# Up projection: the high and the low half of the activations side by side in one 512-column matmul, in two of seven product slots

## The chip, the cores and the metric

The kernel runs on one core of one Trainium2 chip. The metric is the device time of one execution in microseconds (us); the kernel before takes 685.49 us, the median of three runs (685.24 to 686.26).

## The reference

One layer of a decoder trunk on 512 tokens of width 1024 (`SEQ = 512`, `D_MODEL = 1024`, `D_FF = 2816`): two attention branches, a merge, and then the gated MLP whose first matrix product is the one that is changed here.

```python
def _conv_ffn(h, w_up, conv_w, conv_b, w_down):
    u = h @ w_up                       # (512, 1024) @ (1024, 5632)
    a, g = jnp.split(u, 2, axis=-1)    # 2816 columns each
    s = a.shape[1]
    ap = jnp.pad(a, ((0, 0), (CONV_WIDTH - 1, 0), (0, 0)))
    a = ap[:, 0:s] * conv_w[0] + ap[:, 1:s + 1] * conv_w[1] + ap[:, 2:s + 2] * conv_w[2] + conv_b
    return (jax.nn.gelu(a, approximate=False) * g) @ w_down
...
    h2 = _rmsnorm(x, norm2_g[l]) * (1.0 + scale2) + shift2
    x = x + gate2 * _conv_ffn(h2, w_up[l], conv_w[l], conv_b[l], w_down[l])
return _rmsnorm(x, final_g)
```

All arrays are float32.

## The kernel before

The kernel computes the float32 products with float32r matmuls. Every operand is split into a high part (a cast to float32r on ScalarE) and a low part (the rest, a subtraction on VectorE), and a product is three matmuls: high weights times high activations, high weights times low activations, low weights times high activations. In the up projection the weights are the stationary operand, 128x128 each, and the activations are the moving operand, 256 tokens wide (H = 256).

The up projection is a Strassen-Winograd scheme. It works on 11 pairs J = 0 to 10 of 128-column blocks (NPR = 11). For each J the four blocks of weights are the upper and lower half of the 1024 rows for the `a` columns and for the `g` columns, and the four blocks of activations are the two halves of the rows for tokens 0 to 255 ("lo") and 256 to 511 ("hi"). Instead of eight block products there are seven, called p1, m5, m6, p2, m7, p3, p4, and they are issued in this order: one slot each. A slot has, for u = 0 and u = 1 (128 of the pair's 256 output columns each), 4 steps over the rows times 3 matmuls: 24 matmuls in all (`mul_slot`). Then `behind(J, name)` reads the result out of the accumulator memory (PSUM):

- p1 (L1394): ScalarE copies it to `a[lo]`. m5 (L1396): ScalarE copies it to `g2`. m6 (L1398): it has been added onto p1 in PSUM; ScalarE copies the sum to `a[hi]`.
- p2 (L1400): VectorE adds it to `a[lo]`. m7 (L1402): it has been added onto p1 + m6; VectorE subtracts it from `g2`. p3 (L1404): it has been added onto m5; VectorE adds the sum to `a[hi]`. p4 (L1406): it has been added onto p1 + m6 + m7; VectorE multiplies it into the result.

After p3 come the convolution and GELU of this pair (`conv`: bias on ScalarE L1369, two taps on VectorE L1373 and L1374, GELU on ScalarE L1377). At each slot the weights of a later slot are made ready (`prep`): for m6 and p3 a sum of two blocks (L1293, VectorE), then the cast (L1299, ScalarE), then the low part (L1303, VectorE). The high and low weight tiles have three buffers each (WB = 3), so a cast for one slot can start when the slot three before it has been multiplied.

A PSUM bank holds 128 x 512 float32, and an accumulator of the up projection takes half a bank. For each u there are four banks, and `psum(J, name)` says which one a product goes to and in which half of it (h):

```python
    def psum(J, name):
        if name in ("m5", "p3"):
            b, h = bV, J % 2
        elif name == "p2":
            b, h = bX, J % 2
        else:
            b, h = (bU0, bU1)[J % 2], J // 2 % 2
        return [b[u][:, h * H : (h + 1) * H] for u in range(2)]
```

For J = 0, for J = 1 and for the slot p1 of J = 2 the order on VectorE, ScalarE, TensorE and GpSimd is written out by hand: there `mul_slot(2, "p1")` is followed by `mul_slot(1, "p4")`, and `behind(2, "p1")` stands behind `cast_w(2, "m6")`. From the slot m5 of J = 2 on the compiler's scheduler orders the engines: it takes instructions that are ready, those that stand earlier in the program first.

Of the kernel before, what the change touches and what calls it, by code (L numbers as in the profile page):

```python
# [8 lines left out]
F32 = mybir.dt.float32  # L9
F32R = mybir.dt.float32r  # L10
AF = mybir.ActivationFunctionType
# [3 lines left out]
P = 128  # L15
D = 1024
S = 512
# [43 lines left out]
def kernel(  # L61
# [22 lines left out]
    nc = tc.nc  # L84
# [3 lines left out]
    def pool(name, bufs=1, space=None, stack=ctx):  # L88
        kw = {} if space is None else {"space": space}
        return stack.enter_context(tc.tile_pool(name=name, bufs=bufs, reuse_waits="tile", **kw))  # L90

    cpool = pool("const")
    big = pool("big")
# [6 lines left out]
    def fbank(name):  # L100
        return bank("f", 2, [P, S], name)

    def sbank(name, shape=(P, S)):
        return bank("s", 3, list(shape), name)
# [4 lines left out]
    def vbank(name):  # L109
        return bank("v", 1, [P, S], name)  # L110
# [97 lines left out]
        rstd_end(dst, *rstd_start(ssq, n, d, wpool, plus), n, wpool)  # L208


    def parts_of(n):
        a = big.tile([P, 6, S], F32R, tag=f"h{n}A", name=f"hT{n}A")
        b = big.tile([P, 2, S], F32R, tag=f"h{n}B", name=f"hT{n}B")
        return [a[:, k] for k in range(6)] + [b[:, k] for k in range(2)]

    hTh, hTl = parts_of("h"), parts_of("l")
    p1 = ExitStack()
    pp = pool("p1", stack=p1)
    xn = pp.tile([P, NT, D], F32, name="xn")
# [408 lines left out]
    hT = (hTh, hTl)  # L628
# [427 lines left out]
    for s in range(4 * DIFF_HEADS):  # L1056
        h, n = divmod(s, NT)
# [164 lines left out]
            done(t)  # L1222


    bh = big.tile([P, 3, 4, 256], F32R, tag="hhA", name="bh")
    bl = big.tile([P, 3, 4, 256], F32R, tag="hlA", name="bl")
    braw = {}
    oacc = eight("oc")
    wa1 = gpart(2, [P, 2, 4, 256], "wa1")
# [26 lines left out]
    NPR, H = FT // 2, S // 2  # L1256
# [9 lines left out]
    W, R = {}, {(1, f"a1{h + 1}"): wa1[:, h] for h in range(2)}  # L1266
# [58 lines left out]
    with tc.issue_after(first_low[1].ins):  # L1325
# [6 lines left out]
    bU0 = [fbank("up0"), fbank("up1")]  # L1332
    bX = [sbank("up2"), sbank("up3")]
    bU1 = [sbank("up4"), vbank("up5")]
    bV = []
    T = dict(
        p1=(bh[:, 0], bl[:, 0]), p2=(bh[:, 1], bl[:, 1]), p3=(bh[:, 2], bl[:, 2]),
        m5=(tt[0][:, 0], tt[0][:, 1]), m6=(tt[1][:, 0], tt[1][:, 1]), m7=(tt[2][:, 0], tt[2][:, 1]),
        p4=(tt[3][:, 0], tt[3][:, 1]),
    )  # L1340


    def psum(J, name):
        if name in ("m5", "p3"):
            b, h = bV, J % 2
        elif name == "p2":
            b, h = bX, J % 2
        else:
            b, h = (bU0, bU1)[J % 2], J // 2 % 2
        return [b[u][:, h * H : (h + 1) * H] for u in range(2)]  # L1350

    av = {}

    def mul_slot(J, name, us=(0, 1)):
        o = psum(J, name)
        wh, wl = W[J, name]
        bh_, bl_ = T[name]
        for u in us:
            cu = slice(u * P, (u + 1) * P)
            for k in range(4):  # L1360
                for x, (w, b) in enumerate(((wh, bh_), (wh, bl_), (wl, bh_))):
                    nc.tensor.matmul(  # L1362
                        o[u], w[:, k, cu], b[:, k], start=name in ("p1", "m5", "p2") and k == 0 and x == 0,
                        stop=k == 3 and x == 2, skip_group_check=True,
                    )

    def conv_bias(J, u):
# [16 lines left out]
    def behind(J, name):  # L1384
        o = [] if name == "c22" else psum(J, name)
        g2 = g22[:, J % 2] if name in ("m5", "m7", "c22") else None
        if name == "p1":
            av[J] = big.tile([P, 2, S], F32, tag=("hhB", "hlB")[J % 2], name=f"a{J}")
        a = av[J]
        lo, hi = slice(0, H), slice(H, S)  # L1390
        for u in range(2):
            cc = grow(2 * J + u)
            if name == "p1":
                nc.scalar.copy(a[:, u, lo], o[u])  # L1394
            elif name == "m5":
                nc.scalar.copy(g2[:, u], o[u])  # L1396
            elif name == "m6":
                nc.scalar.copy(a[:, u, hi], o[u])  # L1398
            elif name == "p2":
                nc.vector.tensor_add(a[:, u, lo], a[:, u, lo], o[u])  # L1400
            elif name == "m7":
                nc.vector.scalar_tensor_tensor(g2[:, u], g2[:, u], -1.0, o[u], ALU.mult, ALU.subtract)  # L1402
            elif name == "p3":
                nc.vector.tensor_add(a[:, u, hi], a[:, u, hi], o[u])  # L1404
            elif name == "p4":
                nc.vector.scalar_tensor_tensor(cc[:, lo], o[u], -1.0, cc[:, lo], ALU.mult, ALU.mult)  # L1406
            elif name == "c22":
                nc.vector.tensor_mul(cc[:, hi], cc[:, hi], g2[:, u])
        if name == "p4":
            nc.vector.tensor_sub(grow(2 * J)[:, hi], grow(2 * J + 1)[:, hi], grow(2 * J)[:, hi])  # L1410
# [138 lines left out]
    for g in (2, 3):  # L1549
        tps[g] = turn2(0, g)  # L1550
    mul_slot(0, "p1")
    early(2, "vec")
    norm_a(3)
# [6 lines left out]
    early(2, "lo")  # L1560
    early(3, "lo")
    mul_slot(1, "p1", (0,))
    bt = gpart(0, [P, 2, 4, 256], "braw2")
    b12, b22 = bt[:, 0], bt[:, 1]
# [8 lines left out]
    def grow(j):  # L1573
        return gT[j // 4][:, j % 4]
# [5 lines left out]
    g22 = pairs2.rearrange("p (b u n) -> p b u n", b=2, u=2)  # L1580
    tps = {g: turn2(2, g) for g in (0, 1)}
    mul_slot(0, "p2", (0,))
    for g in (0, 1):
        for kk in range(2):
# [20 lines left out]
    for q in (q0, q1):  # L1605
        V.scalar_tensor_tensor(t1n[:, q], t1n[:, q], -1.0, b22[:, q], ALU.mult, ALU.subtract)
        hi_t(1, t1n, q)
    behind(0, "p1")
    nc.scalar.copy(bh[:, 2], b22)
    lo_t(1, t1n, q0)  # L1610
# [3 lines left out]
    cast_w(0, "p3")  # L1614
    V.tensor_sub(bl[:, 2], b22, bh[:, 2].bitcast(F32))
    behind(0, "m5")
    low_w(0, "p3")
    mul_slot(0, "p3")
# [3 lines left out]
    V.scalar_tensor_tensor(b21, t1n, -1.0, b21, ALU.mult, ALU.subtract)  # L1622
    hi_t(3, b21)
    behind(0, "m6")
    low_w(0, "m7")
    lo_t(2, b12)
# [116 lines left out]
        cbuf[c][:, x : x + (2 if g < 5 else 1) * S].rearrange("p (q n) -> p q n", n=S)  # L1743
        for g, (c, x) in enumerate(((0, 0), (0, 1024), (1, 0), (2, 0), (2, 1024), (3, 0)))
    ]
    s2 = big.tile([P, NPR, H], F32, tag="hhA", name="s2")
    s4 = big.tile([P, NPR, H], F32, tag="hlA", name="s4")

    second = {g: big.tile([P, 2, S], F32, tag=t, name=f"b22_{g}") for g, t in enumerate(("hhB", "hlB"))}
    m1 = pairs2.rearrange("p (t n) -> p t n", n=S)  # L1750
# [309 lines left out]
```

## Time and profile before

| | |
|---|---|
| time, median of 3 runs | 685.49 us (685.24 to 686.26) |
| span of the profiled execution, first to last instruction | 684.1 us |
| PE (TensorE matmul) busy | 675.3 us, 99% of the span |
| DVE (VectorE) busy | 564.2 us, 82% |
| ACT (ScalarE) busy | 384.5 us, 56% |
| matmuls of the up projection, line L1362 | first at 348.2 us, last at 571.6 us |
| mean granted TensorE clock | 0.998 |

The page gives the span of the profiled execution and no time of its own beside it; the median of the runs is 1.4 us longer than that span. PE is the matmul row, PEld the load of stationary weights, which runs beside it. In a timeline each line has the start in us, the duration in us, the engine, the line of the kernel, the operation, the tile written and the tiles read, the shapes, the number of merged instructions, and in brackets the idle time of the engine just before and what ended it. The matmuls are pipelined: the duration of one is longer than the distance to the next, and it is the distance that adds up.

### The profile page before, as it was taken

How to read it: one execution, taken by the hardware profiler on the slowest of the kernel's cores; microseconds unless marked ns; L12 is line 12 of the kernel's file. 1: busy time of each engine (PE TensorE's matmuls, PEld its weight loads, DVE VectorE, ACT ScalarE, POOL GpSimd, SP SyncE). 2: the span in 40 equal slices, each digit the busy share in tenths (PEclk: the TensorE clock that was granted, in tenths of full speed). 3: DMA queues.
4: the chain of work that ended last, by engine and by line, in shares of the span. 5: the costliest groups of instructions: out<-in, count | busy, mean ns of one | idle time of the engine just before them, and what ended most of it. 6: DMA issues, size and time to landing. Idle time of an engine off the chain costs nothing. (4 is left out here: it accounts for less than half of the span.)

```text
span 684.1 us, 11125 instructions
## 1 busy us (share of the span) xinstructions
PE 675.3 (99%) x4141; PEld 589.7 (86%) x4141; DVE 564.2 (82%) x1075; ACT 384.5 (56%) x688; POOL 98.5 (14%) x119
## 2 busy tenths in 40 slices
PE   9999999999999999999999999999999999999995
PEld 5887887878888888888899999999999998888885
DVE  4999875988796756974589988888888999979997
ACT  6776774546543223324377665666555665656765
POOL 3000000011012012021030111112120003440300
PEclk9999999999999999999999999999999999999999
DMA  9995422565456885659555788777978647995903
GB/s 304 349 296 181 144 62 64 163 166 162 144 157 181 255 246 158 217 144 345 187 93 109 170 216 212 180 165 207 216 194 216 153 170 186 191 205 146 166 1 123
DMA packets 117142, 123.89 MB, mean 181 GB/s; under 512 B 5063, under 2 KB 94184, under 8 KB 117088
## 3 DMA queue, kind: packets, MB, share of 16 engines
q1 hardware_dynamic: 97246, 95.11, 43.3%
q0 software_dynamic: 19648, 27.79, 24.1%
q8 instruction: 32, 0.52, 0.3%
q10 hardware_dynamic: 194, 0.28, 0.1%
q14 instruction: 22, 0.18, 0.1%
HBM read 118.97 MB, written 2.11 MB: 177 GB/s over the span
## 5 line engine op out<-in xcount | busy, mean ns | idle before, releaser
L1362 PE MATMUL up<-t,m_whi 128*128 128x256 f32 x512 | 93.1, 283 | 0.0
L1362 PEld LDWEIGHTS up<-t,m_whi 128*128 128x128 f32 x512 | 79.9, 192 | 0.0
L1362 PE MATMUL up<-t,m_wlo 128*128 128x256 f32 x256 | 72.4, 283 | 0.0
L1362 PE MATMUL up<-bh,p_whi 128*128 128x256 f32 x232 | 65.7, 283 | 0.0
L1362 PE MATMUL up<-bl,p_whi 128*128 128x256 f32 x232 | 65.7, 283 | 0.0
L1362 PE MATMUL up<-bh,p_wlo 128*128 128x256 f32 x232 | 65.7, 283 | 0.0
L952 POOL DMA_DIRECT2D arow<-arow x28 | 22.5, 804 | 247.8 <-DVE sd L821 123.6
L1362 PEld LDWEIGHTS up<-t,m_wlo 128*128 128x128 f32 x256 | 49.2, 192 | 0.0
L1271 POOL DMA_DIRECT2D s<-in_w_up_dram x21 | 26.9, 1353 | 141.3 <-DMA s<-in_w_up_dram 69.2
L1362 PEld LDWEIGHTS up<-bh,p_whi 128*128 128x128 f32 x232 | 44.5, 192 | 0.0
L1362 PEld LDWEIGHTS up<-bl,p_whi 128*128 128x128 f32 x232 | 44.5, 192 | 0.0
L1362 PEld LDWEIGHTS up<-bh,p_wlo 128*128 128x128 f32 x232 | 44.5, 192 | 0.0
L944 DVE SCALAR_TENSOR_TENSOR arow<-ra,cs,arow 128x512 f32<-128x512 f32 x56 | 41.8, 748 | 0.6
L1299 ACT CAST m_whi<-s 128x1024 fp32r<-128x1024 f32 x31 | 32.4, 1046 | 11.1 <-DVE s L1293 6.3
L1303 DVE TENSOR_TENSOR m_wlo<-s,m_whi 128x1024 fp32r<-128x1024 f32 x31 | 37.8, 1218 | 0.0
L1362 PE MATMUL up<-t,p_whi 128*128 128x256 f32 x176 | 32.2, 283 | 0.0
L1362 PEld LDWEIGHTS up<-t,p_whi 128*128 128x128 f32 x176 | 27.5, 192 | 0.0
L816 ACT ACTIVATE sd<-sd,dmx 128x128 f32<-128x128 f32 (+3 forms) x32 | 17.7, 557 | 17.3 <-DVE dmx L806 17.3
L1369 ACT ACTIVATE gT<-a,cv 128x512 f32<-128x512 f32 x22 | 17.7, 813 | 16.9 <-DVE a L1404 15.8
L1299 ACT CAST p_whi<-wa 128x1024 fp32r<-128x1024 f32 x18 | 18.7, 1041 | 12.6 <-PE up L1362 12.6
L1303 DVE TENSOR_TENSOR p_wlo<-wa,p_whi 128x1024 fp32r<-128x1024 f32 x18 | 22.0, 1222 | 3.8 <-ACT p_whi L1299 3.8
L1362 PE MATMUL up<-t,p_wlo 128*128 128x256 f32 x88 | 24.9, 283 | 0.0
(499 smaller groups left out, 2052.4 us busy)
## 6 DMA issues: line engine op xcount, KB each, us to landing
ra<-in_w_ada_dram SPq DMA_DIRECT2D x32, 512.0 KB, 4.9
wa<-in_w_up_dram SPq DMA_DIRECT2D x22, 512.0 KB, 4.2
s<-in_w_up_dram SPq DMA_DIRECT2D x21, 512.0 KB, 4.7
s<-in_w_up_dram POOLq DMA_DIRECT2D x21, 512.0 KB, 6.9
w<-in_w_in_dram SPq DMA_DIRECT2D x12, 512.0 KB, 5.0
a<-in_w_up_dram SPq DMA_DIRECT2D x11, 512.0 KB, 4.7
b<-in_w_down_dram SPq DMA_DIRECT2D x10, 512.0 KB, 4.2
adaw<-in_w_ada_dram SPq DMA_DIRECT2D x8, 512.0 KB, 6.3
```

Of the source, the lines that this page charges most:

```text
L816: exp = nc.scalar.activation(pm[m], pm[m], AF.Exp, bias=mx[:, m : m + 1], scale=slope, accum_out=ls)
L944: nc.vector.scalar_tensor_tensor(ac, r[:, a], cc, ac, ALU.mult, ALU.add)
L952: nc.gpsimd.dma_start(whole[0:n], whole[n : 2 * n], accum_op=ALU.add)
L1271: nc.gpsimd.dma_start(dst, upblock(*blk), accum_op=ALU.add)
L1299: nc.scalar.copy(W[J, name][0], R[J, SRC[name]])
L1303: nc.vector.tensor_sub(lo, R[J, SRC[name]], hi.bitcast(F32))
L1362: nc.tensor.matmul(o[u], w[:, k, cu], b[:, k], start=name in ("p1", "m5", "p2") and k == 0 and x == 0, stop=k == 3 and x == 2, skip_group_ ...
L1369: nc.scalar.activation(grow(j), av[J][:, u], AF.Identity, bias=cv[:, 66 + j : 67 + j], scale=cv[:, 44 + j : 45 + j])
```

## The change

Nothing changes for J = 0 and J = 1. For J = 2 to 10:

- The high and low activations of p1, p2 and p3 lie in one tile, `bhl`, so that a view of 2 x 256 columns takes both. In the slots p2 and p3 (`mul_beside`) one matmul of 512 columns multiplies the high weights with high and low activations at once, into the two halves of one bank; a second matmul of 256 columns adds low weights times high activations into half 0. A slot of 24 matmuls becomes one of 16, with the same number of columns.
- The result of these slots is the sum of the two halves. Reading it is now a ScalarE copy of half 1 to the destination and a VectorE addition of half 0.
- The banks are dealt out anew. p1, m5, m6 and p3 use `bU0` or `bU1` (by J % 2): p1 and m6 half 1, m5 half 0, p3 both. p2 uses both halves of `bX`. m7 and p4 use `bV`, half J % 2.
- ScalarE seeds two accumulators by writing to PSUM: behind p1 it writes half of p1 into each half of `bX` (128x512, in place of the copy to `a[lo]`), and behind m6 it writes p1 + m6 into the half of `bV` to which m7 will add (in place of the copy to `a[hi]`).
- The tiles of the first half of the layer that held the same memory (`hTA`), and those of the down projection (`s24`), are joined in the same way.

```diff
+    hTA = big.tile([P, 2, 6, S], F32R, tag="hA", name="hTA")
+
+    def parts_of(i, n):
         b = big.tile([P, 2, S], F32R, tag=f"h{n}B", name=f"hT{n}B")
+        return [hTA[:, i, k] for k in range(6)] + [b[:, k] for k in range(2)]
...
+    bhl = big.tile([P, 2, 3, 4, 256], F32R, tag="hA", name="bhl")
+    bh, bl = bhl[:, 0], bhl[:, 1]
...
+    BESIDE = {"p2": 1, "p3": 2}
+
+    def pair(J, name):
+        return bX if name == "p2" else (bU0, bU1)[J % 2]
+
     def psum(J, name):
-        if name in ("m5", "p3"):
+        if J >= 2 and name not in ("m7", "p4"):
+            b, h = pair(J, name), 1 if name in ("p1", "m6") else 0
+        elif J >= 2 or name in ("m5", "p3"):
             b, h = bV, J % 2
         elif name == "p2":
             b, h = bX, J % 2
         else:
-            b, h = (bU0, bU1)[J % 2], J // 2 % 2
+            b, h = (bU0, bU1)[J % 2], 0
         return [b[u][:, h * H : (h + 1) * H] for u in range(2)]
...
+    def mul_beside(J, name):
+        wh, wl = W[J, name]
+        i = BESIDE[name]
+        for u, bk in enumerate(pair(J, name)):
+            cu = slice(u * P, (u + 1) * P)
+            both = bk.rearrange("p (b n) -> p b n", b=2)
+            for k in range(4):
+                nc.tensor.matmul(both, wh[:, k, cu], bhl[:, :, i, k], start=False, stop=k == 3, skip_group_check=True)
+                nc.tensor.matmul(
+                    both[:, 0], wl[:, k, cu], bhl[:, 0, i, k], start=False, stop=k == 3, skip_group_check=True
+                )
+
     def mul_slot(J, name, us=(0, 1)):
+        if J >= 2 and name in BESIDE:
+            return mul_beside(J, name)
...
+        opens = name == "p1" or J == 0 and name in ("m5", "p2")
...
-                        o[u], w[:, k, cu], b[:, k], start=name in ("p1", "m5", "p2") and k == 0 and x == 0,
-                        stop=k == 3 and x == 2, skip_group_check=True,
+                        o[u], w[:, k, cu], b[:, k], start=opens and k == 0 and x == 0, stop=k == 3 and x == 2,
+                        skip_group_check=True,
...
     def behind(J, name):
...
-            if name == "p1":
+            if name == "p1" and J >= 2:
+                nc.scalar.activation(
+                    bX[u].rearrange("p (b n) -> p b n", b=2), o[u].unsqueeze(1).to_broadcast([P, 2, H]), AF.Copy,
+                    scale=0.5,
+                )
+            elif name == "m6" and J >= 2:
+                nc.scalar.copy(psum(J, "m7")[u], o[u])
+            elif name in BESIDE and J >= 2:
+                part = a[:, u, lo if name == "p2" else hi]
+                nc.scalar.copy(part, pair(J, name)[u][:, H:])
+                nc.vector.tensor_add(part, part, o[u])
+            elif name == "p1":
                 nc.scalar.copy(a[:, u, lo], o[u])
...
-    s2 = big.tile([P, NPR, H], F32, tag="hhA", name="s2")
-    s4 = big.tile([P, NPR, H], F32, tag="hlA", name="s4")
+    s24 = big.tile([P, 2, NPR, H], F32, tag="hA", name="s24")
+    s2, s4 = s24[:, 0], s24[:, 1]
```

More of the change, by code (lines that the diff above doesn't have):

```diff
@@ L208, in rstd_m2 @@
         rstd_end(dst, *rstd_start(ssq, n, d, wpool, plus), n, wpool)
-    def parts_of(n):
-        a = big.tile([P, 6, S], F32R, tag=f"h{n}A", name=f"hT{n}A")
+    hTA = big.tile([P, 2, 6, S], F32R, tag="hA", name="hTA")
+    def parts_of(i, n):
         b = big.tile([P, 2, S], F32R, tag=f"h{n}B", name=f"hT{n}B")
-        return [a[:, k] for k in range(6)] + [b[:, k] for k in range(2)]
-    hTh, hTl = parts_of("h"), parts_of("l")
+        return [hTA[:, i, k] for k in range(6)] + [b[:, k] for k in range(2)]
+    hTh, hTl = parts_of(0, "h"), parts_of(1, "l")
     p1 = ExitStack()
@@ L1222, in tok_proj @@
             done(t)
-    bh = big.tile([P, 3, 4, 256], F32R, tag="hhA", name="bh")
-    bl = big.tile([P, 3, 4, 256], F32R, tag="hlA", name="bl")
+    bhl = big.tile([P, 2, 3, 4, 256], F32R, tag="hA", name="bhl")
+    bh, bl = bhl[:, 0], bhl[:, 1]
     braw = {}
```

## The prediction

> **What bounds the kernel now.** I read the page first, for the busy engine:
>
> ```profile
> PE 675.3 (99%) x4141; PEld 589.7 (86%) x4141; DVE 564.2 (82%) x1075; ACT 384.5 (56%) x688; POOL 98.5 (14%) x119
> L1362 PE MATMUL up<-bh,p_whi 128*128 128x256 f32 x232 | 65.7, 283 | 0.0
> ```
>
> Then the sums by stretch, cut at the first matmul of a slot m5 (413.36, below) and at whole pairs from there:
>
> ```profile
> 413.36:433.52 20.16, 20.16 (x171) 20.16 (x170) 17.29 (x25) 11.69 (x18) 2.56 (x2) 1.00 0.85 196
> 534.32:554.48 20.16, 20.16 (x171) 20.16 (x170) 18.29 (x27) 12.68 (x20) 0.00 (x0) 1.00 0.33 95
> ```
>
> The columns are the length, then PE, PEld, DVE, ACT and POOL busy, the granted clock and the DMA share. PE has no gap at all here, the clock is full, VectorE is busy 17.3 to 18.3 of 20.16 us and ScalarE 11.7 to 12.7. So the stage is bound by TensorE, a shorter stream of matmuls shortens the kernel one to one, and so does a stall of TensorE in the other direction. The 283 ns of the page is the length of one pipelined matmul and not what it costs; that is the distance between starts, from the timeline of TensorE around the slots p1, m5 and m6 of J = 3:
>
> ```profile
> 411.80 0.28 PE L1362 MATMUL up<-bh,p_wlo 128*128 128x256 f32 x1
> 411.92 0.28 PE L1362 MATMUL up<-bh,p_whi 128*128 128x256 f32 x1
> 413.24 0.28 PE L1362 MATMUL up<-bh,p_wlo 128*128 128x256 f32 x1
> 413.36 0.40 PE L1362 MATMUL up<-t,m_whi 128*128 128x256 f32 x2
> 414.80 0.40 PE L1362 MATMUL up<-t,m_whi 128*128 128x256 f32 x2
> 416.24 0.40 PE L1362 MATMUL up<-t,m_whi 128*128 128x256 f32 x2
> ```
>
> A matmul of 256 columns every 0.120 us: 12 for one u take 1.44 us (413.36 to 414.80 to 416.24), a slot 2.88, seven slots 20.16. For 512 columns the output projection is the nearest stretch:
>
> ```profile
> 330.17 0.39 PE L1418 MATMUL oc<-wo_whi,mg2h 128*128 128x512 f32 x1
> 330.40 0.39 PE L1419 MATMUL oc<-wo_wlo,mg2h 128*128 128x512 f32 x1
> 330.62 0.39 PE L1418 MATMUL oc<-wo_whi,mg2h 128*128 128x512 f32 x1
> 330.85 0.39 PE L1419 MATMUL oc<-wo_wlo,mg2h 128*128 128x512 f32 x1
> 331.08 0.61 PE L1422 MATMUL oc<-wo_whi,mg2l 128*128 128x512 f32 x2
> 331.53 0.39 PE L1418 MATMUL oc<-wo_whi,mg3h 128*128 128x512 f32 x1
> ```
>
> Six matmuls in 1.36 us, 226.7 ns each. So two of 256 cost 240.0 ns and one of 512 costs 226.7.
>
> **The gain.** Two slots of each J from 2 to 10 join 8 pairs of matmuls: 9 x 2 x 8 = 144 joins of 13.3 ns, 1.92 us in all, or 0.21 us for each J. Two things have no row: a matmul of 512 alternating with one of 256, and a moving operand in two runs of 256. I bound them by nothing and by a further 13.3 ns a matmul (the gain gone, 1.92 us), and take nothing, since both sizes show the same 13.3 ns beyond their columns.
>
> The Trainium skill ("TensorE: Matmul & The Clock Gate", section Back-to-back issue gap) puts the fixed part of a warm matmul at about 2.5 ns beside N/2.4; by that the 144 joins would be worth an estimated 0.4 us. The rows above show 13.3 ns, and I go by them.
>
> **The price: a bank that is read cannot be multiplied into.** Before, a product that is being read lies in another bank than the next slot's. After, p1, m5 and m6 of one J lie in the same bank for each u, in three slots that follow one another: m5 goes to half 0 while ScalarE must read p1 from half 1, m6 to half 1 while ScalarE must read m5 from half 0. Whether that makes TensorE wait depends on whether the program guards halves or whole banks. Two places of the trace tell. In the first, VectorE reads a half that was finished after 6 of 12 matmuls, and starts when all 12 are done; in the second, ScalarE reads one half of a bank of transposes and VectorE the other, and VectorE starts as ScalarE ends its first:
>
> ```profile
> 57.16 0.95 PE L139 MATMUL sw<-ka,qa 64*128 64x128 f32 x12
> 58.14 0.29 DVE L667 CUSTOM_DVE_ANT_0 st<-sw,dsw 128x128 f32<-128x128 f32 x1 [0.97 <-PE sw L139]
> ...
> 353.24 1.02 ACT L1467 ACTIVATE braw<-th,c 128x256 f32<-128x256 f32 x2 [0.23 <-PE th L1457]
> 353.84 1.00 DVE L1465 TENSOR_SCALAR braw<-th,c 128x256 f32<-128x256 f32 x2 [0.66 <-ACT braw L1467]
> ```
>
> So whole banks are guarded, and m5 for u = 0 waits for the reading of p1 for u = 0, m5 for u = 1 for that of u = 1, and so m6 for m5. Each reader has 1.44 us, the matmuls of the other u, before TensorE stands still. What ScalarE does in that time, J = 3, before:
>
> ```profile
> 412.12 0.37 ACT L1394 COPY a<-up 128x256 f32<-128x256 f32 x1 [1.49 <-PE up L1362]
> 412.87 1.05 ACT L1299 CAST m_whi<-s 128x1024 fp32r<-128x1024 f32 x1 [0.38 <-DVE s L1293]
> 413.82 0.63 ACT L1377 ACTIVATE gT<-gT 128x512 f32<-128x512 f32 x1
> 414.36 1.04 ACT L1299 CAST p_whi<-wa 128x1024 fp32r<-128x1024 f32 x1
> 415.29 0.36 ACT L1394 COPY a<-up 128x256 f32<-128x256 f32 x1
> 415.56 0.37 ACT L1396 COPY pairs<-up 128x256 f32<-128x256 f32 x1
> 416.32 1.05 ACT L1299 CAST m_whi<-s 128x1024 fp32r<-128x1024 f32 x1 [0.39 <-PE up L1362]
> 417.27 0.36 ACT L1396 COPY pairs<-up 128x256 f32<-128x256 f32 x1
> 417.88 0.38 ACT L1398 COPY a<-up 128x256 f32<-128x256 f32 x1 [0.24 <-PE up L1362]
> 419.24 1.05 ACT L1299 CAST p_whi<-s 128x1024 fp32r<-128x1024 f32 x1 [0.99 <-PE up L1362]
> 420.20 0.36 ACT L1398 COPY a<-up 128x256 f32<-128x256 f32 x1
> ```
>
> p1 is complete at 413.36, but its second copy (415.29) runs behind the cast for m6, a GELU of the pair before and the cast for p2. All three stand earlier in the program, and the change leaves that so. Today nothing hangs on this copy; after, m5 for u = 1 does.
>
> The seed itself is now 128x512. No row writes ScalarE to PSUM. Below it is bounded by the copy of half the width, above by the bias step; I take the copy of 128x512 out of PSUM, 0.58 us:
>
> ```profile
> L1396 ACT COPY pairs<-up x22: 348/370/381, 363.2 to 558.4; 128x256 f32<-128x256 f32 x22
> L1831 ACT COPY pairs<-dc x2: 575/582/589, 586.6 to 587.1; 128x512 f32<-128x512 f32 x2
> L1369 ACT ACTIVATE gT<-a,cv 128x512 f32<-128x512 f32 x22 | 17.7, 813 | 16.9 <-DVE a L1404 15.8
> ```
>
> For J = 3 to 10, on the clock of J = 3: the seed of u = 0 is done at 412.12 + 0.58 = 412.70, before m5 starts at 413.36: no wait. The seed of u = 1 runs from 415.29 to 415.87; with 0.05 us from one engine to the next (the cast that ends at 420.29 releases VectorE at 420.33 in the row below) m5 for u = 1 starts at 415.92 in place of 414.80: a stall of 1.12 us.
>
> ```profile
> 420.33 1.23 DVE L1303 TENSOR_TENSOR p_wlo<-s,p_whi 128x1024 fp32r<-128x1024 f32 x1 [0.62 <-ACT p_whi L1299]
> ```
>
> m5 then ends at 417.36, and the copy of its u = 0 is long done. Its second copy comes behind the cast for m7, 417.44 + 0.95 + 0.36 = 418.75, and m6 for u = 1 is due at 418.80: nothing, by 0.05 us. m7 needs the seeds behind m6, which come some 1.3 us into the slot p2, 2.8 us long: nothing. p1 of the next J opens the other bank: nothing. So each of these J costs 1.12 - 0.21 = 0.91 us, and eight of them 7.3 us.
>
> For J = 2 the order by hand puts the seeds behind the cast for m6:
>
> ```profile
> 393.01 1.06 ACT L1299 CAST m_whi<-s 128x1024 fp32r<-128x1024 f32 x1 [3.58 <-DVE s L1293]
> 393.97 0.63 ACT L1394 COPY a<-up 128x256 f32<-128x256 f32 x2
> ...
> 393.20 0.40 PE L1362 MATMUL up<-t,m_whi 128*128 128x256 f32 x2
> ```
>
> m5 starts at 393.20 today, from the last row; after, its u = 0 waits for 393.97 + 0.58 + 0.05 = 394.60: 1.40 us. The seed of u = 1 ends by 395.2 and m5 needs it at 396.04: nothing. With the gain, 1.19 us.
>
> **What else moves.**
>
> ```profile
> 414.08 1.22 DVE L1303 TENSOR_TENSOR m_wlo<-s,m_whi 128x1024 fp32r<-128x1024 f32 x1
> ```
>
> ScalarE gets four more copies of 0.37 us and two wider seeds (+0.21 us each), 1.9 us in a period in which it has 7.5 us free. The additions of p2 and p3 wait for those copies, which stand behind a cast; behind the addition on VectorE stand the taps, and the next low weights. These have room: the tightest low part, that of m6, ends at 415.30 for a slot that starts at 416.24, and each stall adds to that. I count nothing. If it goes through to the seed, it is one copy, 0.37 us for each of eight J, 3.0 us. VectorE's work is the same in number. Joining the tiles costs nothing: high and low parts are last read in the same slots.
>
> **Sum.** Over the profiled span of 684.1 us: + 7.3 + 1.2 = 8.5, 692.6 us. The runs' median lies 1.4 us above that span, so 693.9 or 694.0 by rounding; I say 693.9 us.
>
> **The rivals.** (1) Halves are not guarded: the stalls vanish and only the joins are left, 685.5 - 1.9 = 683.6 us, faster. It decides from a stall under 0.2 us a pair on. For it: ScalarE has 7.5 us free in each period. Against it: the four rows above, and J = 2, whose order is fixed. Chance 0.10. By the Trainium skill ("PSUM — Partial Sum Buffer", section PSUM bank collisions raise a hardware error) two engines may not touch one bank at once, disjoint columns included, so a program without the guard would not even run clean; the waits of the four rows fit that.
>
> (2) The scheduler places the second seed earlier. Straight behind p1: no stall from J = 3 on, 685.5 - 1.9 + 1.4 = 685.0 us. Behind the cast for p2 alone: that cast could start at 413.44, the seed at 414.39 and end at 414.97, a stall of 0.2 us, 8 x 0.2 = 1.6 more, 686.6 us. Both are no change. For it: the copy is ready 1.9 us before it runs. Against it: the same order in the same place in each period. Chance 0.15.
>
> (3) It gets worse than the sum: seeds of 0.81 us (9 x 0.23 = 2.1 us more) and the late copies of p3 (3.0 us), 699.0 us. Chance 0.15.
>
> **How the numbers follow.** The forecast case, m5 stalls for 0.6 to 1.2 us, has 0.60. Two tenths of a per cent, about what can be told from no change, are 1.4 us: faster is below 684.1, slower above 686.9. Rival 1 is faster, rival 2 the same, the rest slower: 0.10, 0.15, 0.75. The range from 684.9 to 699.0 leaves out rival 1 and a tail above (3); the forecast case alone spans 689.8 (0.6 us) to 694.6 (1.2 us).
>
> **What would show it.** The changed profile should have 16 matmuls for p2 and p3, with 2.77 us a slot; idle time of TensorE at `m_whi` of m5, ended by the seed of ScalarE, in the middle of the slot, eight times about 1.1 us and once 1.4 at its start; and a period of 21.1 us. If TensorE has no such gap and the period is 19.95, I am wrong by rival 1; if the gap is at m6, or ended by VectorE, the readers' order is wrong.

## The result, and the profile after

The changed kernel takes 698.25 us (median of 5 runs, 697.33 to 699.72), the kernel before 686.04 us on the same chip (685.24 to 687.56): the ratio is 1.018, with a 95% interval of 1.0165 to 1.0195. It is slower by about 12 us. The prediction was 693.9 us. The profiled execution of after has a span of 697.5 us and a time of 699.28 us; against the span of 684.1 us before, 13.4 us are to be explained.

First the page of after, its busy line and two rows of its groups (busy us, mean ns of one, idle time just before and what ended it):

```profile
PE 678.8 (97%) x3997; PEld 583.3 (84%) x3997; DVE 562.9 (81%) x1075; ACT 399.3 (57%) x724; POOL 98.7 (14%) x119
L1369 PE MATMUL up<-bhl,p_whi 128*128 128x512 f32 x144 | 52.0, 398 | 0.0
L1385 PE MATMUL up<-t,m_whi 128*128 128x256 f32 x512 | 95.3, 287 | 4.8 <-ACT up L1417 4.8
```

The 144 joined matmuls are there. Matmul issues fall from 4141 to 3997, yet TensorE counts more busy time than before (675.3 us), and ahead of `m_whi` it now stands idle for the seed on L1417. The waits of TensorE (us in all, times, longest) say the same, and name a second place:

```profile
PE up L1385 <- ACT up L1417: 4.8, 8, 1.2
PE dc L2038 <- ACT gT L1400: 3.6, 1, 3.6
PE xt L433 <- DVE xn L425: 1.3, 1, 1.3
```

`dc` is the accumulator of the down projection, the stage that follows. The prediction had nothing there.

Now the loss by place, from the starts of the first up matmul, the last one and the first `dc` matmul. The up projection starts at 349.2 us instead of 348.2: 1.0 us. It takes 230.5 us to the end of its last matmul instead of 223.6: 6.9 us. Then there is a gap of 3.8 us where before there was none, and from the first `dc` matmul to the end of the span it takes 114.0 instead of 112.3 us: 1.7 us. The sum is 13.4 us. The first item arises in the first half of the layer, where the wait for `xn` above lies, and it comes and goes from run to run: of the kernels below, b_swap, whose first half is that of before, starts its up projection at 347.6 us and has that wait too, at 0.7 us, and e_nojoin, whose first half is that of after, starts it at 347.5 us. So I do not charge it to the change.

**Inside the up projection.** One period (seven slots) and two stretches around the stage's end, as sums by stretch (length, busy time of PE, PEld, DVE, ACT and POOL, granted clock, DMA share, GB/s):

```profile
418.22:439.15 20.93, 20.42 (x152) 19.36 (x152) 17.05 (x25) 13.23 (x22) 2.55 (x2) 1.00 0.79 191
579.70:583.40 3.70, 0.18 (x2) 0.00 (x0) 3.70 (x8) 2.29 (x3) 1.18 (x1) 1.00 1.00 211
583.83:587.24 3.41, 3.41 (x10) 2.64 (x9) 3.41 (x8) 0.00 (x0) 1.18 (x1) 0.50 1.03 244
```

A period is 20.93 us instead of 20.16. The clock is full, VectorE and ScalarE are no busier than forecast, and TensorE has half a microsecond of holes. The timeline of ScalarE and then of TensorE at m5 of J = 3 shows the largest one:

```profile
414.66 0.58 ACT L1417 ACTIVATE up<-up 128x512 f32<-128x512 f32 x1
415.18 1.03 ACT L1300 CAST m_whi<-s 128x1024 fp32r<-128x1024 f32 x1
416.11 1.04 ACT L1300 CAST p_whi<-wa 128x1024 fp32r<-128x1024 f32 x1
417.06 0.62 ACT L1400 ACTIVATE gT<-gT 128x512 f32<-128x512 f32 x1
417.59 0.58 ACT L1417 ACTIVATE up<-up 128x512 f32<-128x512 f32 x1
...
417.20 0.28 PE L1385 MATMUL up<-t,m_wlo 128*128 128x256 f32 x1
417.32 0.40 PE L1369 MATMUL up<-bhl,p_whi 128*128 128x512 f32 x1
418.22 0.39 PE L1385 MATMUL up<-t,m_whi 128*128 128x256 f32 x1 [0.50 <-ACT up L1417]
```

The seed of u = 0 runs at once. The seed of u = 1 runs behind the cast for m6, the cast for p2 and a GELU, as forecast, and ends at 418.17; m5 for u = 1 starts 0.05 us later. (The bracket counts from the modelled end of the matmul before.) What was not forecast is the second row: the scheduler moved the first matmul of p2, whose bank the earlier seed had already filled, into the hole. Without it m5 for u = 1 would have been due at 417.32; it starts at 418.22, 0.90 us later, of which 0.23 us are work.

At J = 2 the order by hand gives the stall that was forecast (ScalarE, then TensorE):

```profile
394.01 1.05 ACT L1300 CAST m_whi<-s 128x1024 fp32r<-128x1024 f32 x1 [3.58 <-DVE s L1294]
394.96 1.06 ACT L1417 ACTIVATE up<-up 128x512 f32<-128x512 f32 x2
...
394.09 0.28 PE L1385 MATMUL up<-t,p_wlo 128*128 128x256 f32 x1
395.59 0.50 PE L1385 MATMUL up<-t,m_whi 128*128 128x256 f32 x2 [1.22 <-ACT up L1417]
```

The last matmul ahead of it is done at 394.21 (start plus 0.12 us), so the hole is 1.38 us.

**The joins.** The timeline of TensorE in the slot p2 of J = 3:

```profile
422.88 0.40 PE L1369 MATMUL up<-bhl,p_whi 128*128 128x512 f32 x1
423.11 0.28 PE L1370 MATMUL up<-bhl,p_wlo 128*128 128x256 f32 x1
423.23 0.40 PE L1369 MATMUL up<-bhl,p_whi 128*128 128x512 f32 x1
423.47 0.28 PE L1370 MATMUL up<-bhl,p_wlo 128*128 128x256 f32 x1
```

A pair takes 0.35 us; the mean over the 136 undisturbed pairs is 352.5 ns, where 226.7 + 120.0 = 346.7 was forecast and three matmuls of 256 take 360.0. A join is worth 7 ns, and 144 of them 1.0 us.

**At the stage's end.** The timeline of after: TensorE around the first matmul of the down projection, and VectorE's read of p4 that ends just ahead of it.

```profile
579.60 0.28 PE L1385 MATMUL up<-t,p_wlo 128*128 128x256 f32 x1
583.50 0.48 PE L2038 MATMUL dc<-m1wh,m1a 128*128 128x512 f32 x1 [3.62 <-ACT gT L1400]
...
582.94 0.41 DVE L1440 SCALAR_TENSOR_TENSOR gT<-up,gT 128x256 f32<-128x256 f32 x1
```

The timeline of VectorE in before, at the read of the same product:

```profile
574.47 0.75 DVE L1406 SCALAR_TENSOR_TENSOR gT<-up,gT 128x256 f32<-128x256 f32 x2
```

The profile puts the gap down to a GELU, the one that this read needs. The read itself ends at 583.35, and the matmul starts 0.15 us later. In before the read is just as late (it ends at 575.22, the first `dc` matmul had started at 571.76), and nobody waits for it. The difference is the bank. The down projection deals out its banks by `dX, dZ, dY, dW = eight("dc")`, and its first pass, m1, multiplies into `dX`, which is the memory of `bV`. Before, p4 of the last pair lay in `bU0`, and the last product in `bV` was p3, read by 569.5. The change put p4 into `bV`. Behind the gap the granted clock is 0.50 for 3.41 us (third window above; 1.00 just before and behind it): from 583.50 on eleven matmuls take 4.18 us, where 226.7 ns each would be 2.49.

### The profile page after: what moved, and what is told of

Same layout as the page of the kernel before. It is cut to its first block, busy times and chain, and to the rows that moved or that the text cites. A ratio compares the mean times of both kernels' runs of the same rounds, so it can differ in the third digit from the quotient of the medians.

```text
span 697.5 us, 10875 instructions
## 1 busy us (share of the span) xinstructions
PE 678.8 (97%) x3997; PEld 583.3 (84%) x3997; DVE 562.9 (81%) x1075; ACT 399.3 (57%) x724; POOL 98.7 (14%) x119
## 5 line engine op out<-in xcount | busy, mean ns | idle before, releaser
L1385 PE MATMUL up<-t,m_whi 128*128 128x256 f32 x512 | 95.3, 287 | 4.8 <-ACT up L1417 4.8
L1369 PE MATMUL up<-bhl,p_whi 128*128 128x512 f32 x144 | 52.0, 398 | 0.0
L1370 PE MATMUL up<-bhl,p_wlo 128*128 128x256 f32 x144 | 40.5, 281 | 0.0
L1385 PE MATMUL up<-bhl,p_whi 128*128 128x256 f32 x176 | 32.2, 283 | 0.0
L1369 PEld LDWEIGHTS up<-bhl,p_whi 128*128 128x128 f32 x144 | 27.1, 188 | 5.4
L1385 PEld LDWEIGHTS up<-bhl,p_whi 128*128 128x128 f32 x176 | 27.5, 192 | 0.0
L1370 PEld LDWEIGHTS up<-bhl,p_wlo 128*128 128x128 f32 x144 | 27.3, 189 | 0.0
L1385 PE MATMUL up<-bhl,p_wlo 128*128 128x256 f32 x88 | 24.9, 283 | 0.0
```

The lines of the kernel that those rows point to most:

```text
L1369: nc.tensor.matmul(both, wh[:, k, cu], bhl[:, :, i, k], start=False, stop=k == 3, skip_group_check=True)
L1370: nc.tensor.matmul(both[:, 0], wl[:, k, cu], bhl[:, 0, i, k], start=False, stop=k == 3, skip_group_check=True)
L1385: nc.tensor.matmul(o[u], w[:, k, cu], b[:, k], start=opens and k == 0 and x == 0, stop=k == 3 and x == 2, skip_group_check=True,)
```

## The experiments

Ratios are to the kernel before on the same chip, 685.26 to 685.41 us in these comparisons.

**Another bank for the first pass.** Two edits of one line, one in each kernel.

```diff
 e_swap: after, with
-    dX, dZ, dY, dW = eight("dc")
+    dW, dZ, dY, dX = eight("dc")
 b_swap: before, with
-    dX, dZ, dY, dW = eight("dc")
+    dZ, dX, dY, dW = eight("dc")
```

The first takes m1 away from the memory in which p4 lies, the second puts m1 of the kernel before on `bU0`, where its p4 lies.

> The changed kernel (698.25 us) with the banks of the down projection dealt out in another order: its first and fourth pass use the banks that bU1 had, which are free since pair 9, and its last two passes those of bV. Theory 1 (the gap of 3.8 us ahead of the first matmul of the down projection is a wait for the bank in which p4 of the last pair still stands to be read, and the low clock behind the gap is its consequence): gap and slow clock go, 3.8 + 1.7 = 5.5 us less, 692.8 us. Theory 2 (the gap is a wait for the activations or for ScalarE, whose GELU the profile names): no change, 698.3 us.

> The kernel before (686.04 us) with the first pass of the down projection in the banks that bU0 had, in which p4 of the last pair still stands to be read there. Theory 1 (the bank of p4 makes the first pass wait): the reading of p4 ends at about 574.9 us in the trace of before and the first pass starts at 571.9, so a gap of some 3 us, and 1.7 us more if the clock falls behind it: 689.0 to 690.8 us. Theory 2 (not the bank): no change, 686.0 us.

The first takes 692.64 us, ratio 1.0112 (1.0094 to 1.013); the second 690.84 us, ratio 1.0074 (1.0062 to 1.0087). The timeline of TensorE in the first:

```profile
581.69 0.28 PE L1385 MATMUL up<-t,p_wlo 128*128 128x256 f32 x1
581.81 0.40 PE L2038 MATMUL dc<-m1wh,m1a 128*128 128x512 f32 x1
582.05 0.40 PE L2038 MATMUL dc<-m1wl,m1a 128*128 128x512 f32 x1
```

No gap, no slow matmuls, and the same 112.3 us to the end as before. From the first up matmul to the end it is 342.8 us where after takes 348.3: 5.5 us less, which are the 3.8 and the 1.7. In the second, the timeline of TensorE:

```profile
571.01 0.28 PE L1362 MATMUL up<-t,p_wlo 128*128 128x256 f32 x1
574.40 0.76 PE L2004 MATMUL dc<-m1wh,m1a 128*128 128x512 f32 x1 [3.12 <-DVE gT L1406]
574.96 0.63 PE L2004 MATMUL dc<-m1wl,m1a 128*128 128x512 f32 x1
```

and the sums of the stretch with the low clock, which begins inside the gap:

```profile
573.33:580.16 6.83, 5.76 (x14) 4.53 (x15) 5.13 (x10) 0.26 (x1) 2.36 (x2) 0.50 0.93 200
```

One line of bank names gives the kernel before such a gap (3.27 us from 571.13), the same low clock (0.50) behind it, and 5.1 us by the ratio, 5.6 by the medians. So both come from the bank and from nothing else in the change. The first kernel's profiled execution had a hole of 2.3 us in the output projection, far ahead of the edit, with a slow clock behind it; that is why its span, 694.1 us, is longer than its median suggests.

**The seed of p1 ahead of the casts.** After, with the seed raised in the scheduler's order from J = 3 on:

```diff
             if name == "p1" and J >= 2:
-                nc.scalar.activation(
+                with tc.high_priority(offset=HP):
+                    nc.scalar.activation(
...
```

> The changed kernel (698.25 us) with the seed behind p1 given priority on ScalarE, so that the second seed stands ahead of the cast for p2 and of a GELU. Theory 1 (the stall of m5 comes from what is queued ahead of the seed): the gap of 0.67 us and the restart of 0.10 us go in seven periods, period 20.93 to 20.1 us, 7 x 0.8 = 5.6 us less, 692.6 us. Theory 2 (any reading of the shared bank makes m5 wait, whatever its place): no change, 698.3 us.

692.79 us, ratio 1.0104 (1.0091 to 1.0118), 5.2 us less than after by the ratios. The waits of TensorE:

```profile
PE dc L2039 <- ACT gT L1400: 3.6, 1, 3.6
PE up L1385 <- ACT up L1418: 1.2, 1, 1.2
```

The sums over one period:

```profile
440.08:460.24 20.16, 20.16 (x155) 19.35 (x154) 17.04 (x25) 13.26 (x22) 2.56 (x2) 1.00 0.75 183
```

Of the eight waits for the seed one is left, that of J = 2, which the order by hand fixes. Seven periods shorter by 0.77 us are 5.4 us, and the stage takes 225.0 us where after takes 230.5, so the stall of m5 is the whole loss inside the period. But the period is that of before, 20.16, although 16 joins should bring 16 x 7 = 0.11 us. The next timeline, of ScalarE and TensorE at m6, shows where that goes:

```profile
438.36 1.05 ACT L1300 CAST m_whi<-s 128x1024 fp32r<-128x1024 f32 x1 [0.36 <-PE up L1385]
439.32 0.37 ACT L1431 COPY pairs<-up 128x256 f32<-128x256 f32 x1
...
439.60 0.28 PE L1385 MATMUL up<-t,m_wlo 128*128 128x256 f32 x1
439.74 0.50 PE L1385 MATMUL up<-t,m_whi 128*128 128x256 f32 x2
440.08 0.28 PE L1385 MATMUL up<-t,m_wlo 128*128 128x256 f32 x1
```

The copy of m5 for u = 1 stands behind the cast for m7 and ends at 439.69; the first matmul of m6 for u = 1 starts at 439.74, some 0.02 us late, and the row after these two matmuls starts at 440.08, where two more steps of 0.12 us would make 439.98. A wait that is over almost at once still costs TensorE 0.10 us here. After has the same at m6, 0.01 us late and 0.10 us lost, in each J from 3 on.

**The joins undone, and two shapes of them.** After with the 512 columns as two matmuls of 256; after with high and low activations side by side in memory, so that the moving operand is one run of 512; and after with the four matmuls of 512 of a u first and the four of 256 behind them:

```diff
 e_nojoin
-                nc.tensor.matmul(both, wh[:, k, cu], bhl[:, :, i, k], start=False, ...)
+                for x in range(2):
+                    nc.tensor.matmul(both[:, x], wh[:, k, cu], bhl[:, x, i, k], start=False, ...)
 e_contig
-    bhl = big.tile([P, 2, 3, 4, 256], F32R, tag="hA", name="bhl")
+    bhl = big.tile([P, 3, 4, 2, 256], F32R, tag="hA", name="bhl")
 e_group
             for k in range(4):
                 nc.tensor.matmul(both, wh[:, k, cu], bhl[:, :, i, k], ...)
+            for k in range(4):
                 nc.tensor.matmul(both[:, 0], wl[:, k, cu], bhl[:, 0, i, k], ...)
```

> The changed kernel (698.25 us) with each matmul of 512 columns split again into two of 256 columns into the same halves; banks, seeds and readers stay. Theory 1 (a join saves 13.3 ns, as the prediction had it): 144 x 13.3 ns = 1.9 us more, 700.2 us. Theory 2 (a pair of 512 and 256 columns takes 353 ns, as the changed profile has it, against 360 for three of 256): 144 x 7 ns = 1.0 us more, 699.3 us. Less if the stall of m5 takes some of it up.

> The changed kernel with the high and low activations of one step laid next to each other, so that the moving operand of the joined matmul is one run of 512 columns and not two runs of 256; nothing else. Read from the trace, where a slot p2 of before took 24 x 120 ns and one of the changed kernel takes 353 ns for 512 + 256 columns. Theory 1 (the two runs cost the missing 6 ns): 346.7 ns a pair, 2.77 us a slot. Theory 2 (the alternation of a matmul of 512 and one of 256 costs it): 353 ns a pair, no change.

> The changed kernel with the four matmuls of 512 columns of one u first and the four of 256 columns behind them, so that the sizes do not alternate; the operand stays in two runs. Theory 1 (two runs): 4 x 226.7 + 4 x 120 ns plus 6 ns for each of the four, 1.41 us for a u, as now. Theory 2 (alternation): 1.39 us for a u or a little over.

Without the joins it takes 699.2 us, ratio 1.0204 (1.019 to 1.0218). Against after's 1.018 the joins are worth 0.24% or some 1.6 us, and the two intervals overlap: 1.0 and 1.9 us cannot be told apart by the time. The traces decide it: the spacing above, and the stage, which takes 231.4 us without the joins and 230.5 with them, 0.9 us less. With one run of 512 (a single execution, 697.93 us) a pair still takes 0.353 us, so the two runs of the operand cost nothing. With the 512s grouped (a single execution, 697.42 us) the timeline of TensorE has:

```profile
422.16 1.09 PE L1369 MATMUL up<-bhl,p_whi 128*128 128x512 f32 x4
423.09 0.63 PE L1371 MATMUL up<-bhl,p_wlo 128*128 128x256 f32 x4
423.56 0.40 PE L1386 MATMUL up<-t,m_whi 128*128 128x256 f32 x2
```

Four of 512 in 0.93 us are 233 ns each, and the four of 256 take 0.47, 1.40 us together. Alternation isn't the cause either: a matmul of 512 costs 233 ns in this stage and 227 in the output projection. Why is open. This order let the scheduler move four matmuls of p2 into the hole at m5 instead of one, and its period is 20.61 us.

**Everything mended.** After with e_swap, e_seed, e_contig and, by hand for J = 2, the seed ahead of the cast:

```diff
+    behind(2, "p1")
     cast_w(2, "m6")
-    behind(2, "p1")
```

> The changed kernel with all that the runs so far point to: banks of the down projection in the other order, priority for the seeds behind p1, the seeds of J = 2 ahead of the cast for m6 in the order written by hand, and the activations laid next to each other. Theory 1 (the loss is the sum of the gap at the down projection, the stalls of m5 and the stall of J = 2, and nothing else): what is left is the restart of 0.10 us in each m6 and the joins, 1.0 to 1.9 us less and 0.9 us more than before: within 0.2 per cent of before. Theory 2 (something else that ScalarE's extra copies or the seeds bring is still hidden under these): slower than before by 2 us or more.

687.19 us, ratio 1.0029 (1.0017 to 1.004): 10 of the 12 us are back, and what is left is still slightly slower than before. The timeline of ScalarE, then of TensorE, at m6 of J = 2:

```profile
397.07 1.05 ACT L1300 CAST m_whi<-s 128x1024 fp32r<-128x1024 f32 x1 [0.18 <-ACT p_whi L1300]
398.02 0.64 ACT L1431 COPY pairs<-up 128x256 f32<-128x256 f32 x2
...
398.44 0.50 PE L1385 MATMUL up<-t,m_whi 128*128 128x256 f32 x2 [0.76 <-ACT pairs L1431]
```

With the seed early, m5's copies of J = 2 stand behind the casts for p2 and m7. m6 was due at 396.94 and starts at 398.44; two matmuls of p2 fill 0.47 us of that, so 1.03 us are lost: the next link of the same chain. The stage takes 224.6 us, and its sum is 223.6 - 1.0 (joins) + 1.03 + 9 x 0.10 = 224.5. The banks shared by p1, m5 and m6 so eat the whole gain even when the order is as good as I could make it.

**The join without the seeds.** Before, with the joins, but with banks that no neighbour shares: p1, m6, m7 and p4 stay where they were; p2 has both halves of `bX`; m5 goes to half 0 of `bV` and p3 to both. No seed; VectorE adds both halves, one after the other. Once with p2 alone (m5 and p3 as before), once with p2 and p3:

```diff
+            if name == "p2" and J >= 2:
+                nc.vector.tensor_add(a[:, u, lo], a[:, u, lo], bX[u][:, :H])
+                nc.vector.tensor_add(a[:, u, lo], a[:, u, lo], bX[u][:, H:])
+            elif name == "p3" and J >= 2:
+                nc.vector.tensor_add(a[:, u, hi], a[:, u, hi], bV[u][:, :H])
+                nc.vector.tensor_add(a[:, u, hi], a[:, u, hi], bV[u][:, H:])
...
```

> The kernel before with the join in the slot p2 alone, for J = 2 to 10, in a bank that no other slot uses; no seeds, the other products keep their banks; VectorE adds both halves of p2 (two more additions of 0.42 us for each J). Operands next to each other. Theory 1 (the joins are worth 7 to 13 ns each, and the whole loss came from seeds and banks): 72 joins, 0.5 to 1.0 us faster than before, no stall of TensorE. Theory 2 (VectorE, with 0.8 us more in each 20.2 us, becomes late): idle time of TensorE ahead of a slot, slower than before.

> The kernel before with both joins, p2 and p3, for J = 2 to 10, and none of the seeds: m5 and p3 have a bank of bV to themselves (m5 in half 0, p3 in both), p2 has bX, and p1, m6, m7 and p4 stay where they are in before. VectorE adds both halves of p2 and of p3 (four more additions of 0.42 us for each J). Theory 1 (a join is worth 7 ns and no two slots that follow one another share a bank): 144 x 7 ns = 1.0 us faster than before, 0.9985 of it. Theory 2 (VectorE, 17.3 to 18.3 of 20.16 us busy, becomes late with 1.5 us more): TensorE idle ahead of a slot, no gain or slower.

p2 alone takes 684.82 us, ratio 0.9992 (0.9983 to 1.0001); both take 685.01 us, ratio 0.9988 (0.9979 to 0.9997). The sum over the period from m5 of J = 3 on in the second:

```profile
413.82:433.87 20.05, 20.05 (x154) 19.30 (x153) 18.52 (x29) 11.69 (x18) 2.55 (x2) 1.00 0.84 195
```

TensorE has no hole, and VectorE carries the four extra additions of a pair with 1.5 us to spare. From m5 of J = 3 to m5 of J = 10 its period is 20.05 us instead of 20.16, the stage 222.6 instead of 223.6 us: 1.0 us, the 144 joins at 7 ns. It is the one version here whose whole interval lies below the kernel before, by about 0.1%. By the time p2 alone cannot be told from it; its stage takes 223.1 us, half of the gain for half of the joins.

## Why the prediction came out as it did

**The direction and its mechanism were right.** Whole banks are guarded. The stall sits where it was put (m5, u = 1), behind the three instructions that were named, with the 0.05 us from seed to matmul; the slots p2 and p3 fell to 16 matmuls. The seed takes 0.58 us, the copy's price. The period's loss goes with the seed's place alone (e_seed).

**Rival 1** (halves not guarded) and **rival 2** (the scheduler places the second seed earlier) are refuted by the rows of m5 at J = 3: the matmul follows the seed's end, and the seed runs behind all three. Rival 2's time, 685.0 us, is also not what an early seed gives: e_seed has it for J = 3 to 10 and takes 692.8 us, 5.5 us of which are the stage's end. **Rival 3** named the size closest, 699.0, with reasons that did not occur: seeds take 0.58 us, not 0.81, and the late copies of p3 stall nothing. The range reached to 699.0 only through this rival, so it is luck that the 698.25 us lie inside it: without the loss at the stage's end the change takes 692.6 us (e_swap), near the forecast.

**Term by term.** The stall of m5 was put at 1.12 us for eight pairs. It is 0.90 with 0.23 of it filled by a matmul of p2, and the hole restarts with the 0.10 us that the sum lacked, there and at m6. Net of the joins a period costs 0.76 us on average, not 0.91, and it occurs for seven pairs: at J = 10 only some 0.12 us are left, net of the joins, so 5.4 us stand against 7.3. J = 2 was put at 1.40 and measured 1.38; small holes and restarts behind it bring that pair to 1.5 us net of its joins, not 1.19 (from where m5 of J = 2 is due, 394.21, to m5 of J = 3 at 415.88 it is 21.67 us instead of 20.16). The forecast that m6 costs "nothing, by 0.05 us" met a copy that ends 0.01 us too late, and the price of a restart. The joins were put at 13.3 ns and are worth 7. Together the up projection was to lose 8.5 us; these terms make 6.9, which is what it lost. The sum also set the runs' median 1.4 us above the span; in after's profiled execution the time lies 1.8 us above its own span (699.28 against 697.5).

**The step that failed** is "What else moves". It went through VectorE's additions, the low weights and the joined tiles, and followed the new banks only from slot to slot inside the up projection. It did not ask who takes the banks over afterwards. That transfer is 5.5 of the 13.4 us, 3.8 as a wait and 1.7 as a slow clock, and it is why the time came out 4.4 us above the forecast, although the stalls that were forecast came out smaller.

## What to carry to other kernels

When a change deals out accumulator banks anew, list for every bank its last reader and the next writer over the whole kernel, the next stage included: here one line of names was worth 5.5 us, as a loss in one kernel and as a mend in the other. Two accumulators in one bank cost nothing here where no product goes into the bank in the slot right behind the one whose result is still to be read (p23); where ScalarE also does casts, that reader is late by as many casts as stand ahead of it. And a merge of matmuls with the same columns saves only the fixed part of each, 7 ns here, so one wait of a microsecond takes back 150 of them.

## What the runs showed of the hardware

**The clock after a gap.** TensorE's granted clock fell to 0.50 with the gaps of 3.27 us (b_swap) and 3.78 us (after). The shortest gap that did so is in the first half of e_swap's profiled execution, where the output projection waits for a low weight; its timeline of TensorE, and the window with the low clock:

```profile
330.68 0.40 PE L1452 MATMUL oc<-wo_whi,mg3h 128*128 128x512 f32 x1
333.17 0.50 PE L1453 MATMUL oc<-wo_wlo,mg3h 128*128 128x512 f32 x1 [2.09 <-DVE wo_wlo L129]
```

```profile
333.57:336.99 3.42, 3.42 (x10) 2.65 (x9) 0.68 (x1) 0.00 (x0) 0.00 (x0) 0.50 0.88 290
```

That gap is 2.26 us (330.68 plus 0.23 to 333.17). The clock stayed at 1.00 behind the holes of 0.7 us (the period's window above) and of 1.4 us (J = 2). What a gap costs afterwards does not follow its length: 2.7 us behind the 3.27 us in b_swap (from the first `dc` matmul to the end), 1.7 behind the 3.78 us in after. It follows the time for which the clock stays low. That is 3.4 us in after and in e_swap, and 6.8 us in b_swap, of which TensorE works 5.8; at half the clock, half of 3.4 and of 5.8 should be lost, 1.7 and 2.9 us. The gaps of 3.7 to 3.8 us in e_seed, e_nojoin and e_contig brought 3.4 us too, the one of 4.15 us in e_group 6.8. The 6.8 us stand in the two runs whose gap reaches 1.1 us into the low stretch; in the other five the gap ends within 0.04 us of its start or earlier. In the 3.4 us ahead of the fall TensorE had been idle for 2.1 us (e_nojoin) to 3.4 us (e_seed) in all seven. No run here varied this by itself. The Trainium skill ("TensorE: Matmul & The Clock Gate", section What's actually happening) puts the fall to half clock after an idle window of about 3.4 us. The traces differ: 2.26 us was enough here.

**The fixed part of a matmul.** At the low clock none is left to see. In b_swap (TensorE's timeline, the number of merged instructions last)

```profile
575.39 1.05 PE L2004 MATMUL dc<-m1wh,m1a 128*128 128x512 f32 x2
580.08 0.43 PE L2004 MATMUL dc<-m1wl,m1a 128*128 128x512 f32 x1
```

there are 11 matmuls of 512 between these two starts, 426 ns each, 0.833 ns a column. That is twice what a column adds at the full clock, 0.417 ns ((226.7 - 120.0) / 256), with nothing over. At the full clock half of the 426 would be 213 ns, and 227 are measured in the output projection, 233 in the up projection. What the 14 and the 20 ns are, and why they differ, no run here shows.

**Restarts.** A wait of TensorE ahead of a slot of the up projection costs 0.10 us beyond the wait itself, in after for the waits of 1.4 and 0.7 us (m5) and of 0.01 us (m6) alike: the second matmul behind it starts 0.22 us after the first instead of 0.12. Why is open.
